# Five small moves of work in a hybrid decoder block: row factors, y operands, MLP operands, a refill

## The chip, the core and the metric

The kernel runs on one core of a Trainium2 chip. The metric is the device time of one execution in microseconds (us). A core has TensorE (PE in the profile, with its weight loads as PEld), VectorE (DVE), ScalarE (ACT), GpSimd (POOL) and SyncE (SP), which work side by side and wait for each other by semaphores, and 16 DMA engines. Matrix products land in PSUM. Each engine runs its own instructions in their order, so an instruction that waits holds up all that stand behind it on that engine.

## The reference

One decoder layer on x of 1 x 2048 x 1024 in float32; W_in has 3584 columns, the MLP 4096 hidden columns.

```python
h = rmsnorm(x, norm_mix_g)
u = h @ w_in                                  # split into gate_b, gate_c, v, x_r, g
y_conv = gate_b * causal_dwconv(gate_c * v, conv_w)
xr = causal_dwconv(x_r, rnn_conv_w) + rnn_conv_b
r = sigmoid(block_diag(xr, w_a) + b_a);  i = sigmoid(block_diag(xr, w_x) + b_x)
log_a = -8 * r * softplus(-lambda);  a = exp(log_a)
s_t = a_t * s_(t-1) + sqrt(1 - a_t^2) * i * xr          # the RG-LRU, a scan over time
y_rnn = s * gelu(g)
x = x + concat[rmsnorm(y_conv, g_norm_conv), rmsnorm(y_rnn, g_norm_rnn)] @ w_out
x = x + square(relu(rmsnorm(x, norm_mlp_g) @ w_mlp_in)) @ w_mlp_out
out = rmsnorm(x, final_norm_g)
```

## The kernel before

**Precision.** Every large product is made from three passes over operands split into a high and a low part: `round_off` makes the high part by a cast on ScalarE (L172) and the low part by a subtraction on VectorE (L173). So each weight tile and each activation tile costs one instruction on each of the two engines before TensorE can use it. Names end in `_hi` and `_lo`; an operand of the MLP is called `H`.

**Halves and stages.** The 2048 rows are worked in two halves of two blocks of 512 rows (`b = 0` and `b = 2` in the loop of `block_kernel`). Each half has the same stages:

1. The input projection and the two mixers. For b = 0 this is `mixers_plain`, product by product; for b = 2 `mixers_blocks`, where seven block products stand for eight (Strassen's way; the products are called 1, 2, 6, 5, 7, 3, 4 in the order in which they are run). The RG-LRU comes in units of 128 columns (`Lru`: `conv`, `gate`, `scan`, `out`). `Late` holds the last unit of a pair, whose gate and scan are put off into the next product; `between` runs these steps for the last pair of all, inside the next stage.
2. The output projection: `w_out_conv` for the rows' convolution part (twice, for the two row blocks), then `OutRows` for the recurrent part. Products go into PSUM tiles `po`; VectorE adds them to x (`add_rows`, tile x from po, L1231).
3. The MLP's first product: `Up`, 56 block products counted by `n`, with the seven operands H of 1, 2, 6, 5, 7, 3, 4. Results leave PSUM into `snap` tiles by ScalarE copies or VectorE adds (L1069, L1078).
4. The MLP's second product: `Down` (tile dn), and the last norm.

**The start.** The rows' norm factors are known only after squares of x have been summed. They are turned into a row of factors (`firsts[k].factors()`), spread over 128 partitions by a matmul of a diagonal with ones (`diag`, `bc`, L370), and copied into `R` by ScalarE (L405). `drain_x` (L720) and `drain_g` (L723) multiply product results by R on VectorE and so free their PSUM tiles: start_x and ps_x for x, ps_g for g. `col_products` makes the 48 matmuls of one column block against one block of rows and takes a function `halfway`, which it calls between them; the second spread already goes that way. The stores of kept weights (`d_ws`, on POOL's queue) are released by R (`issue_after(seen)`).

**The y operands.** y of the convolution part is stored in `d_yA`, fetched by `fetch_y` (tile y, two row blocks apart) and split by `conv_operands` into y_hi (ScalarE, L652) and y_lo (VectorE, L653).

**What sets the order.** On TensorE the order is the program's own from the first w_out on (`manual_schedule`) and in `mixers_blocks`; in `mixers_plain`, and on all other engines throughout, a scheduler orders instructions, with the code's order as its base. The PSUM pool has four tiles of 128 x 2 x 512. SP's queue carries most loads and some stores, POOL's queue the stores `d_ws`, `d_wk`, `d_u`, ACT's queue the stores `d_y`.

Of the kernel before, what the change touches and what calls it, by code (L numbers as in the profile page):

```python
# [61 lines left out]
def block_kernel(  # L62
# [618 lines left out]
    def mixers_plain(h):  # L681
        mix = Mix()
        late = None
        nxt = [Rows(2 + k, rs_next[:, k, :]) for k in range(2)]
        us = {}
        R = temp("R")
        R2 = None

        def over(t, blk):
            return t[:, blk : blk + 1, :].broadcast_to([P, 2, TB])  # L690

        def both(nm, drain, blks=range(2), w=None):
            w = w or take(nm)
            for blk in blks:
                drain(blk, col_products(nm, w, h[blk]))
            return w

        def around(nm, drain, steps):
            w = both(nm, drain, (0,))
            if steps:  # L700
                if nm == "c0":
                    late.u0.gate(late.gw)
                    late.u0.scan()
                else:
                    late.gate()
            both(nm, drain, (1,), w)
            if nm == "c0":
                late.gate()
            if steps:
                late.scan()  # L710

        for n in SEQUENCE:
            if n < 4:
                pr = n
                u0, u1 = Lru(2 * pr), Lru(2 * pr + 1)
                xin = new_xin(pr)
                g = wide("g")

                def drain_x(blk, ps):
                    V.tensor_mul(block(xin, blk, 3), ps, over(R, blk))  # L720

                def drain_g(blk, ps):
                    V.tensor_mul(block(g, blk), ps, over(R, blk))  # L723
                    nc.scalar.activation(block(g, blk), block(g, blk), AF.Gelu_apprx_tanh)

                if pr == 0:
                    pss = []
                    wg = both("g0", lambda blk, ps: pss.append(ps), (0,))
                    with tc.issue_after(prepare_second()):
                        for k in range(4):  # L730
                            firsts[0].part(k)
                    firsts[0].factors()
                    both("x0", lambda blk, ps: pss.append(ps), (1,), w_first)
                    psR = psum("bc")
                    firsts[0].spread(R[:, 0, :], psR[:, 0, :])
                    seen = nc.gpsimd.tensor_copy(warm, R[:, 0, 0:1]).ins
                    with tc.issue_after(seen):
                        for m, i, pair in held:
                            kept[m, i] = [spill_r("ws", t, nc.gpsimd) for t in pair]
                    split_kept = spilled[0]  # L740
                    drain_x(0, start_x)
                    for k in range(4):
                        firsts[1].part(k)
                    firsts[1].factors()
                    pss.append(
                        col_products(
                            "g0", wg, h[1], lambda: firsts[1].spread(R[:, 1, :], psR[:, 1, :])
                        )
                    )
                    drain_x(1, pss[1])  # L750
                    drain_g(0, pss[0])
                else:
                    around("x%d" % pr, drain_x, late)
                    wg = None
                gw = load_gate(pr)
                keep_halo(pr, xin)
                u0.conv(xin)
                if late:
                    late.out()
                if pr == 3:  # L760
                    fetched = [fetch_y(mix.ys["A"], q, 0) for q in range(2)]
                if pr:
                    wg = both("g%d" % pr, drain_g, (0,), take("g%d" % pr, 1 + pr // 3))
                u1.conv(xin)
                last = latest[0]
                if pr == 3:
                    keep_sums(n)
                    rA = stats(mix.acc["A"], 512, "A")
                if pr:
                    both("g%d" % pr, drain_g, (1,), wg)  # L770
                else:
                    drain_g(1, pss[2])
                if pr == 3:
                    ysA = conv_operands(fetched)
                if pr:
                    u0.gate(gw)
                    u0.scan()
                late = Late(mix, u0, u1, g, gw)
                if pr < 3:
                    with tc.issue_after(last), tc.issue_after(split_kept):  # L780
                        keep_sums(n)
                continue
            if n < 6:
                pr = n - 4
                if R2 is None:
                    R2 = temp("R2")
                    nc.scalar.activation(R2, R, AF.Square)
                gc = wide("gc")
                around(
                    "c%d" % pr,  # L790
                    lambda blk, ps: V.tensor_mul(block(gc, blk), ps, over(R2, blk)),
                    late,
                )
                if late:
                    late.out()
                    late = None
                cv = new_cv(pr)
                both(
                    "v%d" % pr,
                    lambda blk, ps: V.tensor_mul(block(cv, blk, 2), ps, block(gc, blk)),  # L800
                )
                u = conv_short(pr, cv)
                for blk in range(2):
                    V.tensor_mul(block(u, blk), block(u, blk), over(R, blk))
                us[pr] = spill("u", u, nc.gpsimd)
                for k in range(4):
                    nxt[pr].part(k)
                nxt[pr].factors()
            else:
                for pr in range(2):  # L810
                    u = refill_u(us[pr])
                    around(
                        "b%d" % pr, lambda blk, ps: V.tensor_mul(block(u, blk), ps, block(u, blk)), late
                    )
                    if late:
                        late.out()
                        late = None
                    mix.conv(u)
            keep_sums(n)

        def between(t):
            if t == 0:
                late.gate()
                late.scan()
            if t == 1:
                late.out()

        return mix, rA, ysA, between
# [100 lines left out]
    class InGate(In):  # L929

        def drain(self, i):
            def gated(u, blk, a):
                V.tensor_mul(block(u, blk), a, block(u, blk))

            def snap(t, ps):
                nc.scalar.copy(t, ps)
                return t

            def plus(t, ps):
                V.tensor_add(t, ps, t)  # L940
                return t

            if i == 1:
                self.u0 = refill_u(self.us[0])
                self.t = wide("snap")
                snap(block(self.t, 0), self.x)
            elif i == 2:
                gated(self.u0, 0, plus(block(self.t, 0), self.y))
            elif i == 6:
                self.u1 = refill_u(self.us[1])  # L950
                snap(block(self.t, 1), self.x)
            elif i == 5:
                snap(block(self.t, 0), self.w)
            elif i == 7:
                gated(self.u1, 1, plus(block(self.t, 0), self.x))
            elif i == 3:
                gated(self.u0, 1, plus(block(self.t, 1), self.w))
            elif i == 4:
                gated(self.u1, 0, self.x)
# [377 lines left out]
    for b in range(0, NB, 2):  # L1337
# [8 lines left out]
        with tc.manual_schedule(engines={nc.tensor.engine}):  # L1346
# [1 line left out]
            ahead = 0 if b else 1  # L1348
            ws = [take("oA0", ahead), take("oA1", ahead)]

            nextA = []

            def during(t):
                if t == 0:
                    nextA.extend(fetch_y(mix.ys["A"], q, 1) for q in range(2))
                between(t)
                if t == 0:
                    ysA.extend(conv_operands(nextA))
                if t == 2:
                    load_unit(cursor[0])  # L1360
# [75 lines left out]
        with tc.manual_schedule(engines={nc.tensor.engine}):  # L1436
# [6 lines left out]
            for n in range(-LEAD1, len(seq)):  # L1443
# [26 lines left out]
                    rest(2, xs[0])  # L1470
                if n == 1:
                    rest(3, xs[1])
                if n == 2:
                    for q in range(2):
                        V.tensor_tensor(raw1[q], raw1[2 + q], raw1[q], SUB)
                    ops.put(ops.begin(7), raw1[:2])
                if n == 3:
                    ops.put(ops.begin(3), raw1[2:])
                if n == 4:
                    ops.put(ops.begin(4), raw0[2:])  # L1480
                if s == NS - 1 and i in (5, 7, 3, 4):
                    m = (5, 7, 3, 4).index(i)
# [128 lines left out]
```

## Time and profile before

| | |
|---|---|
| Time, median of 3 runs | 2160.62 us (2160.02 to 2161.12) |
| The profiled execution | 2160.86 us, span 2159.1 us |
| Busy: PE | 2125.7 us, 9488 matmuls |
| Busy: DVE, ACT, POOL | 1481.7, 966.7, 184.8 us |
| DMA | 472.51 MB, mean 219 GB/s |

The span is the time from the first to the last record of the profiled execution, and all times of the timeline count from its start. A row of the timeline has the start in us, the busy us, the engine, the line of the code, the operation with the tiles out<-in, the shape and the number of instructions in the row; in brackets stands the idle time of the engine ahead of it, with the instruction that ended it. A row of the waits has total us, times and the longest. A row of the windows has the stretch, its length, the busy us of PE, PEld, DVE, ACT and POOL, the granted clock of PE (1.00 is full), the share of the DMA engines and GB/s. A matmul of 128 x 512 is shown as 0.39 us long, but the next starts before it ends.

### The profile page before, as it was taken

The page shows a single profiled execution, that of the slowest core. Times are in us where ns is not written, and L with a number is a line of the kernel's source. Part 1 is how long each engine was busy: PE and PEld are TensorE (multiplying, and loading weights), DVE is VectorE, ACT ScalarE, POOL GpSimd, SP SyncE. Part 2 cuts the span into 40 slices and gives each one's busy share as a digit, 9 for nine tenths or more (in the row PEclk, how much of TensorE's full clock was granted, in tenths as well). Part 3 has the DMA queues.
Part 4 walks back from the last instruction along what each step waited for, and adds up shares of the span by engine and source line. Part 5 has one row for each costly group of instructions (what it writes and reads, how often), then busy time and mean ns, then how long its engine had stood idle before and what let it go on. Part 6 is the DMA issues. An engine that isn't in the chain of part 4 may idle for free. (4 is left out here: it accounts for less than half of the span.)

```text
span 2159.1 us, 25110 instructions
## 1 busy us (share of the span) xinstructions
PE 2125.7 (98%) x9488; PEld 1745.3 (81%) x9488; DVE 1481.7 (69%) x1726; ACT 966.7 (45%) x1218; POOL 184.8 (9%) x335
## 2 busy tenths in 40 slices
PE   9999999999999999999999999999999999999998
PEld 7888887887888878888887887778888888888886
DVE  5887877569787876577746567595886665644456
ACT  6745537354333234453536447474533233433333
POOL 1121210000111100000121121000000000000000
PEclk9999999999999999999999999999999999999999
DMA  8755755342887789699573574654144444876431
GB/s 294 292 201 211 279 188 176 128 156 95 298 307 257 285 335 409 260 401 336 191 256 107 189 265 159 241 185 166 49 161 161 156 156 176 338 290 228 157 137 78
DMA packets 180904, 472.51 MB, mean 219 GB/s; under 512 B 15664, under 2 KB 62768, under 8 KB 179760
## 3 DMA queue, kind: packets, MB, share of 16 engines
q1 hardware_dynamic: 141104, 328.30, 42.0%
q0 software_dynamic: 36800, 133.19, 16.5%
q10 hardware_dynamic: 2880, 9.44, 1.2%
q8 instruction: 74, 1.21, 0.2%
q14 instruction: 46, 0.38, 0.0%
HBM read 308.33 MB, written 162.53 MB: 218 GB/s over the span
## 5 line engine op out<-in xcount | busy, mean ns | idle before, releaser
L870 PE MATMUL up<-H,w_hi 128*128 128x512 f32 x1792 | 552.5, 390 | 4.2 <-DVE snap L1078 3.4
L173 DVE TENSOR_TENSOR w_lo<-w,w_hi 128x1024 fp32r<-128x1024 f32 x208 | 253.2, 1222 | 273.8 <-issue 170.9
L870 PEld LDWEIGHTS up<-H,w_hi 128*128 128x128 f32 x1792 | 335.6, 188 | 74.8 <-ACT H L172 4.2
L1172 PE MATMUL dn<-w_lo,z_hi 128*128 128x512 f32 x896 | 348.8, 389 | 2.0 <-DVE w_lo L173 2.0
L1172 PE MATMUL dn<-w_hi,z_hi 128*128 128x512 f32 x896 | 349.2, 390 | 1.6 <-DVE x L1549 1.6
L870 PE MATMUL up<-H,w_lo 128*128 128x512 f32 x896 | 348.6, 389 | 0.0
L1172 PE MATMUL dn<-w_hi,z_lo 128*128 128x512 f32 x896 | 348.6, 389 | 0.0
L172 ACT CAST z_hi<-z 128x1024 fp32r<-128x1024 f32 x112 | 117.9, 1053 | 260.9 <-PE dn L1172 244.7
L172 ACT CAST w_hi<-w 128x1024 fp32r<-128x1024 f32 x208 | 216.0, 1049 | 30.2 <-DVE w L1051 14.6
L870 PE MATMUL in<-H,wr 128*128 128x512 f32 x888 | 203.2, 390 | 0.4 <-ACT g L892 0.4
L1172 PEld LDWEIGHTS dn<-w_lo,z_hi 128*128 128x128 f32 x896 | 168.2, 188 | 38.0 <-DVE w_lo L173 2.8
L1172 PEld LDWEIGHTS dn<-w_hi,z_hi 128*128 128x128 f32 x896 | 168.2, 188 | 37.8 <-DVE x L1549 2.4
L870 PEld LDWEIGHTS up<-H,w_lo 128*128 128x128 f32 x896 | 168.2, 188 | 35.2
L1172 PEld LDWEIGHTS dn<-w_hi,z_lo 128*128 128x128 f32 x896 | 168.2, 188 | 34.6
L870 PEld LDWEIGHTS in<-H,wr 128*128 128x128 f32 x888 | 166.4, 188 | 36.0 <-ACT g L892 0.8
L173 DVE TENSOR_TENSOR z_lo<-z,z_hi 128x1024 fp32r<-128x1024 f32 x112 | 136.6, 1219 | 19.9 <-ACT z_hi L172 18.6
L1065 ACT COPY snap<-up 128x1024 f32<-128x1024 f32 x48 | 48.8, 1016 | 184.6 <-PE up L870 184.6
L258 PE MATMUL po<-w_hi,y_hi 128*128 128x512 f32 x384 | 122.1, 400 | 4.0 <-ACT w_hi L172 3.0
L258 PE MATMUL po<-w_hi,y_lo 128*128 128x512 f32 x384 | 120.0, 394 | 3.3 <-DVE y_lo L653 3.3
L258 PE MATMUL po<-w_lo,y_hi 128*128 128x512 f32 x384 | 119.9, 394 | 0.2 <-DVE w_lo L173 0.2
L173 DVE TENSOR_TENSOR w_lo<-raw,w_hi 128x1024 fp32r<-128x1024 f32 (+1 forms) x62 | 73.1, 1186 | 47.9 <-issue 25.3
L172 ACT CAST w_hi<-raw 128x1024 fp32r<-128x1024 f32 (+1 forms) x62 | 62.7, 1019 | 88.4 <-PE ps_x L235 23.8
(265 smaller groups left out, 3088.7 us busy)
## 6 DMA issues: line engine op xcount, KB each, us to landing
z<-d_z SPq DMA_DIRECT2D x112, 512.0 KB, 7.4
w<-in_w_mlp_out_dram SPq DMA_DIRECT2D x80, 512.0 KB, 6.1
wr<-d_ws POOLq DMA_DIRECT2D x74, 512.0 KB, 6.4
w<-in_w_mlp_in_dram SPq DMA_DIRECT2D x64, 512.0 KB, 4.9
d_z<-snap SPq DMA_DIRECT2D x64, 512.0 KB, 3.0
w<-d_w SPq DMA_DIRECT2D x64, 512.0 KB, 4.7
d_z<-z SPq DMA_DIRECT2D x48, 512.0 KB, 2.9
d_ws<-w_hi POOLq DMA_DIRECT2D x37, 512.0 KB, 6.8
```

The source lines that it names most:

```text
L172: nc.scalar.copy(hi, src)
L173: latest[0] = V.tensor_tensor(lo, src, hi.bitcast(F32), SUB).ins
L258: nc.tensor.matmul(ps[:, half, :], ys[:, j, t * P : (t + 1) * P], ws[j][:, 0, half * 512 : (half + 1) * 512], start=first and i == 0, stop ...
L870: nc.tensor.matmul(ps[:, j, :], ws[:, k, j * P : (j + 1) * P], hs(k), start=i in (1, 2, 5) and k == 0 and n == 0, stop=k == 3 and n == len ...
L1065: nc.scalar.copy(t, ps)
L1172: nc.tensor.matmul(ps[t // 2][:, t % 2, :], zs[:, p, t * P : (t + 1) * P], ws[:, p, :], start=i in (1, 2, 5) and a == 0 and p == 0 and n == 0,
```

## The change

Of the five pieces that it is named for, four stand in the diff. The first spread of the row factors moves into the second row block's x product. In the first half's first w_out, the next y are split ahead of `between`. In the MLP, the operands of products 7, 3 and 4 are made behind block products 3, 5 and 6 and not 2, 3 and 4. In the gate's drain, the refill of the second u moves from product 6 to product 5, which is run right behind it. For the last LRU units' buffers, both files have the same line.

```diff
@@ mixers_plain, the first pair
                     firsts[0].factors()
-                    both("x0", lambda blk, ps: pss.append(ps), (1,), w_first)
                     psR = psum("bc")
-                    firsts[0].spread(R[:, 0, :], psR[:, 0, :])
+                    pss.append(
+                        col_products(
+                            "x0",
+                            w_first,
+                            h[1],
+                            lambda: firsts[0].spread(R[:, 0, :], psR[:, 0, :]),
+                        )
+                    )
                     seen = nc.gpsimd.tensor_copy(warm, R[:, 0, 0:1]).ins
@@ the gate's drain
             elif i == 6:
-                self.u1 = refill_u(self.us[1])
                 snap(block(self.t, 1), self.x)
             elif i == 5:
+                self.u1 = refill_u(self.us[1])
                 snap(block(self.t, 0), self.w)
@@ block_kernel, the first w_out_conv
-            nextA = []
 
             def during(t):
                 if t == 0:
-                    nextA.extend(fetch_y(mix.ys["A"], q, 1) for q in range(2))
+                    nextA = [fetch_y(mix.ys["A"], q, 1) for q in range(2)]
+                    if not b:
+                        ysA.extend(conv_operands(nextA))
                 between(t)
-                if t == 0:
+                if t == 0 and b:
                     ysA.extend(conv_operands(nextA))
@@ block_kernel, Up
-                if n == 2:
+                if n == 3:
                     for q in range(2):
                         V.tensor_tensor(raw1[q], raw1[2 + q], raw1[q], SUB)
                     ops.put(ops.begin(7), raw1[:2])
-                if n == 3:
+                if n == 5:
                     ops.put(ops.begin(3), raw1[2:])
-                if n == 4:
+                if n == 6:
                     ops.put(ops.begin(4), raw0[2:])
```

What the change does to the engines' orders is shown at three places. In the changed file lines move down by 6 behind the first edit and by 7 behind the MLP's.

At the start, TensorE, where ps_x is followed by ps_g (h_379 to h_386 are the second row block's parts). Before:

```order
L235 MATMUL ps_x<-h_385,w_hi 128x512
L235 MATMUL ps_x<-h_386,w_hi 128x512
L235 MATMUL ps_x<-h_385,w_lo 128x512
L370 MATMUL bc<-diag,ones 128x512
L235 MATMUL ps_g<-h_367,w_hi 128x512
L235 MATMUL ps_g<-h_368,w_hi 128x512
```

Now:

```order
L235 MATMUL ps_x<-h_379,w_lo 128x512
L370 MATMUL bc<-diag,ones 128x512
L235 MATMUL ps_x<-h_379,w_hi 128x512
L235 MATMUL ps_x<-h_380,w_hi 128x512
L235 MATMUL ps_x<-h_379,w_lo 128x512
L235 MATMUL ps_x<-h_385,w_hi 128x512
L235 MATMUL ps_x<-h_386,w_hi 128x512
L235 MATMUL ps_x<-h_385,w_lo 128x512
L235 MATMUL ps_x<-h_385,w_hi 128x512
L235 MATMUL ps_x<-h_386,w_hi 128x512
L235 MATMUL ps_x<-h_385,w_lo 128x512
L235 MATMUL ps_g<-h_367,w_hi 128x512
```

The matmuls of the first spread (bc) moved ahead of the last nine of ps_x. The second bc moved too, from behind 24 matmuls of the ps_g that follows to behind 41.

At the same place, ScalarE (xq are squares, rs_s the root for the second row block's factors). Before:

```order
L397 ACTIVATE xq,s_1_115<-xq 128x512 x2
L325 ACTIVATE rs_s<-rs_a 128x4
L405 COPY R<-bc 128x512
L172 CAST gate<-gate_raw 128x256
L724 ACT_TABLE_LOAD
L724 ACTIVATE g<-g 128x2x512
L172 CAST w_hi<-raw 128x1024 x2
L405 COPY R<-bc 128x512
```

Now:

```order
L405 COPY R<-bc 128x512
L397 ACTIVATE xq,s_1_115<-xq 128x512 x2
L724 ACT_TABLE_LOAD
L724 ACTIVATE g<-g 128x2x512
L325 ACT_TABLE_LOAD
L325 ACTIVATE rs_s<-rs_a 128x4
L172 CAST w_hi<-raw 128x1024
L172 CAST gate<-gate_raw 128x256
L172 CAST w_hi<-raw 128x1024
L405 COPY R<-bc 128x512
L172 CAST w_hi<-raw 128x1024
L724 ACT_TABLE_LOAD
```

The root for the second factors moved behind the first gelu (L724), and there are two more table loads.

In the first w_out of the first half, VectorE (x<-po are the drains, gi, xr and r the last unit's gate). Before:

```order
L535 TENSOR_SCALAR r<-xr 128x1024
L1231 SCALAR_TENSOR_TENSOR x<-po,yr_A,x 128x512
L536 SCALAR_TENSOR_TENSOR xr<-xr 128x1024
L530 TENSOR_TENSOR gi<-gi,xr 128x1024
L1231 SCALAR_TENSOR_TENSOR x<-po,yr_A,x 128x512 x2
L538 TENSOR_TENSOR gi<-gi,xr 128x1024
L539 SCALAR_TENSOR_TENSOR xr<-r,state,gi 128x1024
L544 TENSOR_TENSOR gi<-xr,g 128x1024
L653 SCALAR_TENSOR_TENSOR y_lo<-y,prm,y_hi 128x512
```

Now:

```order
L535 TENSOR_SCALAR r<-xr 128x1024
L653 SCALAR_TENSOR_TENSOR y_lo<-y,prm,y_hi 128x512
L536 SCALAR_TENSOR_TENSOR xr<-xr 128x1024
L653 SCALAR_TENSOR_TENSOR y_lo<-y,prm,y_hi 128x512 x3
L1237 SCALAR_TENSOR_TENSOR x<-po,yr_A,x 128x512
L538 TENSOR_TENSOR gi<-gi,xr 128x1024
L1237 SCALAR_TENSOR_TENSOR x<-po,yr_A,x 128x512
L539 SCALAR_TENSOR_TENSOR xr<-r,state,gi 128x1024
L1237 SCALAR_TENSOR_TENSOR x<-po,yr_A,x 128x512
L544 TENSOR_TENSOR gi<-xr,g 128x1024
L530 TENSOR_TENSOR gi<-gi,xr 128x1024
```

The four y_lo moved ahead of a drain of po, and the second unit's gi (L530) behind the first unit's scan (L539). On ScalarE the four y_hi stand ahead of the second unit's gate in the same way.

In the MLP's start of each half, VectorE (raw_3506 and raw_3507 make the operand H of product 7; numbers are of the first half). Before:

```order
L1048 TENSOR_TENSOR s_3897<-w_3502,w_3524 128x1024
L1475 TENSOR_TENSOR raw_3506<-raw_3508,raw_3506 128x1024
L1049 TENSOR_TENSOR w_3524<-w_3524 128x1024
L1475 TENSOR_TENSOR raw_3507<-raw_3509,raw_3507 128x1024
L1051 TENSOR_TENSOR w_3502<-w_3524,w_3502 128x1024
L173 TENSOR_TENSOR H_3932<-raw_3506,H_3930 128x1024
L173 TENSOR_TENSOR H_3933<-raw_3507,H_3931 128x1024
L173 TENSOR_TENSOR w_lo<-w_3521,w_hi 128x1024
L1078 TENSOR_TENSOR snap<-up,snap 128x1024
```

Now:

```order
L1054 TENSOR_TENSOR s_3897<-w_3502,w_3524 128x1024
L1482 TENSOR_TENSOR raw_3506<-raw_3508,raw_3506 128x1024
L1055 TENSOR_TENSOR w_3524<-w_3524 128x1024
L173 TENSOR_TENSOR w_lo<-w_3521,w_hi 128x1024
L1057 TENSOR_TENSOR w_3502<-w_3524,w_3502 128x1024
L1084 TENSOR_TENSOR snap<-up,snap 128x1024
L1482 TENSOR_TENSOR raw_3507<-raw_3509,raw_3507 128x1024
L1075 SCALAR_TENSOR_TENSOR snap<-snap 128x1024
L173 TENSOR_TENSOR H_3965<-raw_3506,H_3963 128x1024
L173 TENSOR_TENSOR H_3966<-raw_3507,H_3964 128x1024
```

The snap (L1078, now L1084) moved ahead of one raw and of both H. Where the refill of u stands (SP's rows of u from d_u), no engine's order has changed.

## The prediction, made before the changed kernel had run

> **What bounds the kernel now.** I read the busy table of the page first, then the waits of TensorE (PE), then the granted clock, then the timeline around each wait that the change touches.
>
> ```profile
> span 2159.1 us, 25110 instructions
> PE 2125.7 (98%) x9488; PEld 1745.3 (81%) x9488; DVE 1481.7 (69%) x1726; ACT 966.7 (45%) x1218; POOL 184.8 (9%) x335
> ```
>
> PE is busy for 98% of the span and the change leaves its 9488 matmuls as they are, so only PE's idle time, and time at a lower clock, can be won or lost. The idle time has names:
>
> ```profile
> PE up L870 <- DVE snap L1078: 3.4, 2, 1.7
> PE po L258 <- DVE y_lo L653: 3.3, 3, 1.9
> PE po L258 <- ACT w_hi L172: 3.0, 1, 3.0
> PE dn L1172 <- DVE w_lo L173: 2.0, 1, 2.0
> PE ps_g L235 <- DVE xr_in L720: 2.0, 1, 2.0
> ```
>
> Columns: total us, times, longest. Edit 3 touches the first row, edit 2 the second, edit 1 the fifth: 8.7 us together. The windows view gives the granted clock (PEclk) in the stretch after that fifth wait, and in two others:
>
> ```profile
> 44.00:49.00 5.00, 4.97 (x15) 3.99 (x16) 2.29 (x7) 2.72 (x4) 2.51 (x5) 0.66 1.00 392
> ...
> 392.00:398.00 6.00, 5.49 (x23) 4.56 (x24) 1.91 (x15) 1.46 (x3) 0.00 (x0) 0.72 0.41 121
> 1386.00:1394.00 8.00, 6.79 (x16) 4.96 (x17) 5.77 (x5) 5.05 (x5) 0.00 (x0) 0.57 0.26 84
> ```
>
> At 0.66 for 5 us, (1 − 0.66) × 5 = 1.7 us are lost beside the 2.0 idle.
>
> **Edit 1, the first spread.** R, the row factors' copy, is made from a bc matmul. R feeds xr_in on VectorE (DVE), which frees the PSUM buffer that ps_g wants. The timeline of PE, then of ACT, then of DVE around it:
>
> ```profile
> 37.84 0.39 PE L235 MATMUL ps_x<-h,w_hi 128*128 128x512 f32 x1
> ...
> 40.78 0.40 PE L235 MATMUL ps_x<-h,w_lo 128*128 128x512 f32 x1
> 41.02 1.02 PE L370 MATMUL bc<-diag,ones 128*128 128x512 f32 x2
> 44.03 0.72 PE L235 MATMUL ps_g<-h,w_hi 128*128 128x512 f32 x2 [1.99 <-DVE xr_in L720]
> ...
> 51.21 1.02 PE L370 MATMUL bc<-diag,ones 128*128 128x512 f32 x2
> ...
> 57.54 0.39 PE L235 MATMUL ps_c<-h_hi,w_hi 128*128 128x512 f32 x1
> 42.13 0.59 ACT L405 COPY R<-bc 128x512 f32<-128x512 f32 x1 [6.42 <-PE bc L370]
> ...
> 34.37 0.62 ACT L397 ACTIVATE xq<-xq 128x512 f32<-128x512 f32 x1
> 45.21 1.06 ACT L724 ACTIVATE g<-g 128x1024 f32<-128x1024 f32 x1 [0.89 <-DVE g L723]
> 42.75 1.22 DVE L720 TENSOR_TENSOR xr_in<-start_x,R 128x1024 f32<-128x1024 f32 x1 [6.23 <-ACT R L405]
> ...
> 45.10 0.86 DVE L362 TENSOR_SCALAR diag<-ident,rs_x 128x128 f32<-128x128 f32 x4
> ...
> 51.23 2.36 DVE L173 TENSOR_TENSOR w_lo<-raw,w_hi 128x1024 fp32r<-128x1024 f32 x2 [4.94 <-issue]
> ```
>
> Thirteen matmuls lie between 37.84 and 40.78: 0.226 us each at full clock. The order of the changed kernel has 9 ps_x matmuls behind bc, so bc starts 9 × 0.226 = 2.0 us earlier, at 39.0. The same chain (copy 1.1 after bc starts, xr_in 0.6 later, 1.22 long) then ends at 41.9, and PE has finished ps_x and bc at 42.0 (44.03 − 1.99): the idle goes. I take the 1.7 of low clock as going with it, since it stands right behind it. Together 3.7; PE drains a little at the changeover, 0.2. Gain 3.5, ps_c at 54.0. If the low clock stays, the gain is 1.8.
>
> The cover is thinner behind it: bc's second matmul group moves from behind 24 ps_g matmuls to behind 41, so to 42.0 + 41 × 0.226 = 51.3. Its diag must be there. ScalarE (ACT) now runs the R copy to 40.7, two squares (34.37: 0.62 each) to 42.0, the gelu table, g (1.06), the sqrt table back, and the root that the factors need: 42.0 + 1.28 + 1.06 + 1.28 = 45.6 (a table load is 1.28 in the next fence). These are two table loads more than before. VectorE's small steps take about 1 us, then diag pieces alternate with two w_lo (1.2 each), which want ps_g's 24th matmul (47.5) done: diag complete at about 50.5, 0.8 us ahead of PE. If that cover is gone, PE waits by the excess. The Trainium skill, "ScalarE: Activation LUTs", What ACT_TABLE_LOAD costs, says that every switch costs about 1.28 us for the load and 1.38 us for a drain, 2.66 in all; two switches would bring the diag to about 53.3, a wait of 2.0 on PE, and edit 1 would be worth 1.5 by it, an estimate. The trace agrees on the load and shows less of a drain: the activation stands 0.01 us behind the load in the next fence (343.29 + 1.28, then 344.58).
>
> The kept weights' stores are released by R as well, so they leave 2 us earlier with it. No wait of PE stands in the waits view that they would end.
>
> **Edit 2, y operands in the first w_out.** In the first half (b = 0) the four next y are split ahead of the last unit's gate instead of between its steps. The DMA view of the fetch (KB each, us to landing), then the timeline of ACT, PE and SP's queue:
>
> ```profile
> y<-d_yA SPq DMA_DIRECT2D x4, 256.0 KB, 7.7
> 343.29 1.28 ACT L533 ACT_TABLE_LOAD   x1
> 344.58 1.15 ACT L533 ACTIVATE r<-r,sp 128x1024 f32<-128x1024 f32 x1
> ...
> 350.43 1.11 ACT L523 ACTIVATE gi<-psri,prm 64x1024 f32<-64x1024 f32 x1
> ...
> 356.29 0.71 ACT L652 ACTIVATE y_hi<-y,prm 128x512 fp32r<-128x512 f32 x1
> 359.62 0.73 PE L258 MATMUL po<-w_hi,y_lo 128*128 128x512 f32 x2 [1.23 <-DVE y_lo L653]
> ...
> 363.15 0.73 PE L258 MATMUL po<-w_hi,y_lo 128*128 128x512 f32 x2 [1.88 <-DVE y_lo L653]
> ...
> 351.88 0.62 PE L258 MATMUL po<-w_hi,y_hi 128*128 128x512 f32 x2
> 337.80 2.30 SPq L127 DMA_DIRECT2D y<-d_yA  x4
> ```
>
> The four loads go out between 337.8 and 340.1; with 7.7 us each they land between 345.5 and 348. Now y_hi follows the r of 344.58: four of 0.7, 345.75 to 348.7. VectorE's y_lo follow each, done by 352. PE wants the first at 358.4 (359.62 − 1.23), so all three waits go: 3.3 idle, and about 0.15 more for each restart (below), 3.7. What is late next: the gate (table, r, gi, r, gi) runs after y_hi and a root, to 356.9 instead of 351.5, and PSUM comes free later. PE wants the next buffer at the 351.88 row; VectorE, which does three y_lo ahead of that drain, gives it at about 352.6: a new wait of 0.7. Gain 3.0. If that buffer is the gate's instead, PE waits for the second gi, at about 354.7, 2.8 us, and the gain is 0.9.
>
> **Edit 3, MLP operands 7, 3, 4, in both halves.** VectorE makes the H of block product 7 right ahead of the snap that frees PSUM. The timeline of DVE, then of PE, and a later row of DVE:
>
> ```profile
> 501.40 1.22 DVE L1475 TENSOR_TENSOR raw<-raw,raw 128x1024 f32<-128x1024 f32 x1
> ...
> 505.94 2.35 DVE L173 TENSOR_TENSOR H<-raw,H 128x1024 fp32r<-128x1024 f32 x2
> 508.21 1.22 DVE L173 TENSOR_TENSOR w_lo<-w,w_hi 128x1024 fp32r<-128x1024 f32 x1
> 509.35 1.22 DVE L1078 TENSOR_TENSOR snap<-up,snap 128x1024 f32<-128x1024 f32 x1
> 508.62 0.39 PE L870 MATMUL up<-H,w_lo 128*128 128x512 f32 x1
> 510.71 0.70 PE L870 MATMUL up<-H,w_hi 128*128 128x512 f32 x2 [1.70 <-DVE snap L1078]
> 528.87 1.23 DVE L1048 TENSOR_TENSOR s<-w,w 128x1024 f32<-128x1024 f32 x1 [3.74 <-DMA w<-in_w_mlp_in_dram]
> ```
>
> The start-to-start loss is 510.71 − 508.62 − 0.23 = 1.86, 0.16 over the idle shown. In the new order one raw and the two H stand behind the snap. The two H hold VectorE from 505.94 to 508.21, 2.27, and a raw half of that: the snap starts 3.4 earlier, at 505.9, ends at 507.1, and PE wants the buffer at 508.85. The wait goes with 1.7 to spare, and its twin in the second half too (the waits row has two, 3.4 together): 2 × 1.85 = 3.7. The H pieces come later. H of 7 should be ready by about 512, of 3 by 520, of 4 by 524; at 11 us a block product, PE uses 7 first at about 525 and 4 at 536. So these cost nothing, short of the cover of over 10 us going. The next w_lo may come up to 0.3 late at about 560, in each half; I count 0, and 0.6 as the other end.
>
> **Edit 4 and the fifth piece.** Moving the refill of u in the loop leaves every engine's and queue's order and waits in that region as they were: 0. The fifth, the last units' buffers, has no line in the diff: 0.
>
> **The sum.** 3.5 + 3.0 + 3.7 = 10.2. The profiled execution took 2160.86 us, 1.8 around its span and 0.24 over the median of 2160.62. Against the first it gives 2150.7, against the median 2150.4. I say 2150.5.
>
> **The rivals.** *New waits take most of it.* The diag is 2 us late and brings back the low clock (edit 1 worth −0.2), and PSUM waits for the gate (edit 2 worth 0.9); with the 0.6 at edit 3 the sum is −0.2 + 0.9 + 3.1 = 3.8: 2156.8. One of the two alone leaves 6.5 to 8: 2152.5 to 2154. For it: 0.8 us of cover. Against: every term behind that 0.8 is a measured row.
>
> *The gain is absorbed.* If the two waits on w_lo and w_hi in the second fence end at a fixed time because loads arrive then, everything earlier is lost there; only the second half of edit 3 is behind both: 1.9, 2158.7. For it: VectorE waits for loads of weights in the MLP (528.87). Against: these loads are issued as buffers come free, which PE paces, so they move too.
>
> *The clock goes another way.* Two other low-clock stretches cost 1.7 and 3.4 us by the windows above, (1 − 0.72) × 6 and (1 − 0.57) × 8, the latter in part its idle. If the shift in time takes PE past them, 3 to 5 more are won: about 2146.5. Against: the idle stays. Other waits of 1.7 to 1.9 us (363.15, 510.71) have no low clock behind them, so it is partly a matter of when. The Trainium skill, "TensorE: Matmul & The Clock Gate", Part 1: The HAM clock gate, has the clock halve after an idle window of about 3.4 us that runs freely; by it no wait here is long enough, and edit 1 would have no low clock to win. The trace, 0.66 behind 1.99 idle, does not bear that out.
>
> *Slower.* The last unit's y is stored and fetched again late, since its gate runs later:
>
> ```profile
> 372.82 0.33 ACTq L131 DMA_DIRECT2D d_y<-gi  x1
> ...
> 387.89 1.38 ACT L652 ACTIVATE y_hi<-y,prm 128x512 fp32r<-128x512 f32 x2 [2.92 <-DMA y<-d_y]
> ```
>
> I put the store about 5.7 later, at 378.5; with 2.6 for its landing and 2.6 for the fetch (my estimate, from DMA times at this place in the trace) the last y is there at about 384, against PE's need 3 us earlier than now, at about 388: it holds with about 1 us left after the splits. Each us beyond costs PE one. Slower by 0.2% needs 10.2 + 4.3 lost there, so a store 15 us later still: if the scan chain were held behind the whole column block. Then about 2166.
>
> **How the numbers follow.** 0.2%, 4.3 us, is about what a measurement of this kernel tells from no change. The forecast 0.68; one new wait 0.10; two 0.05; absorbed 0.07; the clock's luck 0.06; slower 0.04. The forecast's own terms have ends of 1.8 to 3.5, 0.9 to 3.7 and 3.1 to 3.7, so 2149.7 to 2154.8; I reach below to the clock's luck, 2145.5, and above to the bound of faster, 2156.3, which leaves out the double wait, the absorbed and the slower case, 0.16. Faster: 0.68 + 0.10 + 0.06 = 0.84; same: 0.05 + 0.07 = 0.12; slower 0.04.
>
> **What would show it.** Right: ps_g starts by 42.2 with no idle and PEclk at 1.0 behind it; ps_c at about 54; no wait on y_lo around 356 and one under 1 us on a drain of po about 7 us earlier; no wait on snap L1078 (L1084 in the new numbering) at about 505 and 1555; PE's total idle down by some 8. Wrong: a wait of PE on diag near 51, on gi near 351, or on a late y near 385; waits on w_lo or w_hi at the starts of Down and of the second w_out that have grown.

## The result, and the profile after

| | median us | runs | against before |
|---|---|---|---|
| before | 2160.87 | 4 | |
| after | 2149.51 | 4 (2147.82 to 2153.81) | 0.9947 (0.9931 to 0.9963) |
| before, beside e5 | 2159.89 | 23 | |
| after, once more (e5) | 2149.07 | 6 | 0.9945 (0.9932 to 0.9958) |

The change makes the kernel about 11 us faster; 10.2 were forecast. The profiled execution of after took 2147.82 us, 13.0 less than the profiled one of before, so the two traces show about 2 us more than the medians do. The ratios leave out three disturbed executions: 7641.73 us in e1, 2366.12 in e5 and 10180.74 in e8. The page of after:

```profile
span 2146.0 us, 25111 instructions
PE 2123.7 (99%) x9488; PEld 1746.1 (81%) x9488; DVE 1480.2 (69%) x1726; ACT 969.0 (45%) x1220; POOL 184.7 (9%) x335
```

The waits of TensorE in after, with the same columns as before:

```profile
PE po L258 <- ACT w_hi L172: 3.0, 1, 3.0
PE psri L509 <- DVE xr_lo L173: 1.8, 2, 1.0
PE dn L1178 <- DVE x L1556: 1.6, 2, 0.8
...
PE po L258 <- DVE x L1237: 0.7, 1, 0.7
```

The rows on snap L1078, on y_lo and on xr_in are gone, and one of 0.7 on a drain of po is new. Two more rows of before are gone, whose going the prediction did not forecast: the 2.0 on w_lo at the start of Down, and this one, on the snap L1086 near 707:

```profile
PE up L870 <- DVE snap L1086: 0.7, 1, 0.7
```

All rows of PE's waits together come to 24.4 us in before and 13.4 in after.

Laying each matmul of after beside the same one of before gives where the 13.0 us lie: +1.2 at the start (from 3 to 8 us 28 matmuls fall where before has 41; this differs from run to run), −3.6 by ps_c, −2.9 over the first w_out, −2.0 at each of the two snap waits, −3.4 in the first half's MLP from about 565 to 797, and −0.4 at a wait of statistics near 1449.

At the start, the timeline of PE in after:

```profile
40.18 1.02 PE L370 MATMUL bc<-diag,ones 128*128 128x512 f32 x2
...
42.89 0.39 PE L235 MATMUL ps_x<-h,w_lo 128*128 128x512 f32 x1
43.19 0.74 PE L235 MATMUL ps_g<-h,w_hi 128*128 128x512 f32 x2
...
52.67 1.02 PE L370 MATMUL bc<-diag,ones 128*128 128x512 f32 x2
...
55.15 0.39 PE L235 MATMUL ps_c<-h_hi,w_hi 128*128 128x512 f32 x1
```

and the timeline of ACT there:

```profile
43.13 1.28 ACT L724 ACT_TABLE_LOAD   x1
44.43 1.06 ACT L724 ACTIVATE g<-g 128x1024 f32<-128x1024 f32 x1
45.51 1.28 ACT L325 ACT_TABLE_LOAD   x1
46.80 0.21 ACT L325 ACTIVATE rs_s<-rs_a 128x4 f32<-128x4 f32 x1
```

ps_g starts 0.30 us behind the last ps_x, 0.07 more than the 0.226 of one matmul to the next. Each table load is followed by its activation 0.01 to 0.02 us after its end. The windows of after, at the start and at the two later stretches of low clock:

```profile
44.00:49.00 5.00, 5.00 (x23) 4.13 (x22) 1.80 (x10) 4.96 (x7) 1.76 (x4) 1.00 1.00 389
...
385.00:395.00 10.00, 9.49 (x43) 7.86 (x42) 5.65 (x19) 3.87 (x6) 0.00 (x0) 0.83 0.67 229
1376.00:1386.00 10.00, 9.53 (x30) 6.92 (x32) 5.63 (x6) 4.31 (x5) 0.00 (x0) 0.66 0.44 138
```

The low clock behind the first wait has gone; the two others stand. In the first w_out and at the MLP's start, DVE in after:

```profile
347.55 2.07 DVE L653 SCALAR_TENSOR_TENSOR y_lo<-y,prm,y_hi 128x512 fp32r<-128x512 f32 x3
349.54 0.74 DVE L1237 SCALAR_TENSOR_TENSOR x<-po,yr_A,x 128x512 f32<-128x512 f32 x1
...
500.59 1.22 DVE L1084 TENSOR_TENSOR snap<-up,snap 128x1024 f32<-128x1024 f32 x1
```

and PE:

```profile
350.33 0.73 PE L258 MATMUL po<-w_hi,y_hi 128*128 128x512 f32 x2 [0.71 <-DVE x L1237]
...
503.51 0.61 PE L876 MATMUL up<-H,w_hi 128*128 128x512 f32 x2
```

The three y_lo hold up one drain, and PE waits 0.71 for it. The snap that frees the MLP's buffer now ends at 501.81, 1.7 before PE comes to it at 503.51.

### The profile page after: what moved, and what is told of

Its sections match the earlier page's. It is cut to its first block, busy times and chain, and to the rows that moved or that the text cites. A ratio compares the mean times of both kernels' runs of the same rounds, so it can differ in the third digit from the quotient of the medians.

```text
span 2146.0 us, 25111 instructions
## 1 busy us (share of the span) xinstructions
PE 2123.7 (99%) x9488; PEld 1746.1 (81%) x9488; DVE 1480.2 (69%) x1726; ACT 969.0 (45%) x1220; POOL 184.7 (9%) x335
## 3 DMA queue, kind: packets, MB, share of 16 engines
q8 instruction: 74, 1.21, 0.2%
```

## The experiments

Two theories. The first: each edit is worth its own waits, and these add up to the result. The second: there is more in the result than the waits named, since the loads and sums of the second MLP weights (`w2_sums`) changed as well, and the gains of different places depend on each other. The runs of the kernel before beside each set have medians of 2160.05 (33 runs), 2159.89 (23) and 2160.10 (27). The standard deviation of one run is 2 us (the 83 runs lie between 2155.3 and 2165.8), so ratios carry about 0.1%, 2 us. The brackets are 95% intervals.

**e1, edit 1 alone.** The change's first hunk (a hunk is one block of the diff), nothing else.

> Only the first spread is moved into the x product (edit 1); all else as before. Theory: the 1.99 us wait on xr_in and the low clock behind it go, -3.6 us, so about 2157.2; the waits of the MLP's first half (snap L1078 1.70 near 510, snap L1086 0.70 near 707, w_lo 2.03 near 797) stand as before. Rival: those later waits shrink because TensorE comes earlier, up to 2 us more, about 2155.

Measured: 2159.54 us, ratio 1.000 (0.9989 to 1.0011): no gain that can be seen, and 3.6 lies outside the interval. In its trace the local gain is there: counted from the first matmuls, ps_c comes 3.6 us earlier. Later it is given back. Windows of e1:

```profile
44.00:49.00 5.00, 5.00 (x23) 4.12 (x22) 1.80 (x10) 4.00 (x6) 1.54 (x3) 1.00 1.00 387
361.00:366.00 5.00, 5.00 (x16) 3.59 (x15) 4.57 (x7) 1.06 (x1) 0.00 (x0) 0.66 0.55 189
1450.00:1455.00 5.00, 5.00 (x16) 3.91 (x16) 4.56 (x15) 3.22 (x5) 0.00 (x0) 0.66 0.71 247
```

and the waits of its MLP:

```profile
PE dn L1178 <- DVE w_lo L173: 3.2, 1, 3.2
```

Two other stretches run at low clock, 1.7 us lost in each, at places where the profile of before has full clock:

```profile
363.00:368.00 5.00, 4.69 (x19) 3.60 (x20) 5.00 (x8) 1.06 (x1) 0.00 (x0) 1.00 0.83 297
1450.00:1455.00 5.00, 5.00 (x22) 4.15 (x23) 5.00 (x15) 3.80 (x7) 0.00 (x0) 1.00 0.64 217
```

And the wait on w_lo is 1.2 longer. The later waits did not shrink, so the rival fails as well.

**e2, edit 2 alone.** The change's hunk in the first w_out.

> Only the y operands of the first half's first w_out are split early (edit 2). Theory: the three waits on y_lo (3.3 us idle, 3.9 by start times) go, one wait of about 0.7 on a drain of po comes, -2.8 us, about 2158.0; the waits near 510, 707 and 797 stand. Rival: they shrink, to about 2156.

Measured: 2160.07 us, ratio 1.0001 (0.9992 to 1.0011). The trace has the three waits gone and the new one of 0.7. The expected 2.8 lies outside this interval too. The theory's figure fails here as at e1.

**e3, edit 3 alone.** The three conditions on n.

> Only the MLP operands 7, 3 and 4 are made later (edit 3). Theory: the two waits on snap L1078 go (-3.7), and the waits near 565, 707 and 797 go with them (-3.5), because the loads of the second MLP weights stand earlier in SP's queue and the chain of their sums on VectorE starts earlier: -7.2 us, about 2153.6. Rival: the later waits went because the whole stage came earlier by edits 1 and 2; then they stand here, -3.7 us, about 2157.1.

Measured: 2154.99 us, ratio 0.9977 (0.9968 to 0.9986), −3.0 to −6.9 us. Both snap waits are gone. The waits on snap L1086 and on w_lo are still in its trace:

```profile
PE dn L1172 <- DVE w_lo L173: 1.5, 1, 1.5
PE up L870 <- DVE snap L1086: 0.7, 1, 0.7
```

So they do not go with edit 3; the theory's −7.2 is outside the interval, the rival's −3.7 inside.

**e4, edit 4 alone.**

> Only the refill of u is moved to product 5 (edit 4). The orders of all engines and queues are those of before, so both theories expect no difference: 2160.8 us, within 1 us. What it differs by shows what run to run noise does to a median.

Measured: 2159.29 us, ratio 1.0001 (0.9992 to 1.001). No effect. Its use is as a second look at the kernel before. The wait at the start is there, in PE's timeline:

```profile
44.80 0.73 PE L235 MATMUL ps_g<-h,w_hi 128*128 128x512 f32 x2 [1.99 <-DVE xr_in L720]
```

but the window behind it is at full clock, where before had 0.66:

```profile
45.00:50.00 5.00, 5.00 (x23) 4.13 (x23) 2.07 (x6) 2.78 (x4) 2.38 (x5) 1.00 1.00 392
```

The wait on w_lo at Down's start is 0.8 here, against 2.0. The engines' orders are the same in both traces, and yet they differ by 1.7 of low clock and 1.2 of wait, 2.9 us in things that nothing has changed.

**e5, all edits once more.**

> The changed kernel once more, with more runs and another profile. If the waits near 565, 707 and 797 (2.9 us before, none in the first profile after) went because of the change, they are absent here too and the median is some 11 us under before. Rival: they vary from run to run with the loads of the second MLP weights (2.7 us together in the profile before, 3.7, 2.3, 2.2 and 1.6 in the four single edits); then they are back here, up to 2 to 3 us, and the median is 8 to 9 under before.

Measured: 2149.07 us, ratio 0.9945 (0.9932 to 0.9958). A wait on w_lo is back in the MLP:

```profile
PE dn L1178 <- DVE w_lo L173: 1.6, 1, 1.6
```

The median is the one expected if the change had removed these waits (−11), the trace is the rival's: their absence in the first profile was in part chance.

**e6, edits 1, 2 and 4.** The change without the conditions on n.

> Edits 1, 2 and 4, without the MLP operands of edit 3. If gains add by TensorE's idle time: -2.0 -2.6 idle and nothing from the clock, -4.6 us. If the two single results (0.0 each) are all there is: 0 to -1 us. If the low clock at the start counts too: -6.4 us. The wait on snap near 505 stands, 1.7.

Measured: 2155.38 us, ratio 0.9976 (0.9967 to 0.9986), −3.1 to −7.1 us. Its trace is no better than e1's or e2's in the MLP:

```profile
PE up L876 <- DVE snap L1092: 2.7, 2, 2.4
PE dn L1178 <- DVE w_lo L173: 2.1, 1, 2.1
```

Together the two edits gain the 4.6 of their idle, apart they gained nothing that shows. With e3, −5.2 and −5.0 make −10.2, against −11 for all: these two parts add up.

**e7 and e8, the sums moved.** Each job of `w2_sums` one block product earlier, or later, on top of the change:

```diff
-                if more and n > 7 and n % 3 == 2:
-                    w2_sums(n // 3 - 2)
+                if more and 6 < n < 55 and n % 3 == 1:      # e7
+                    w2_sums(n // 3 - 2)
+                if more and n > 8 and n % 3 == 0:           # e8
+                    w2_sums(n // 3 - 3)
```

> The changed kernel with each job of the second MLP weights' sums (w2_sums) issued one block product earlier. If the last job's load, which VectorE waits for ahead of the first w_lo of Down, is what makes the wait near 797, that wait is gone in every run: 1 to 2 us less than the changed kernel. Rival: that wait comes from the first casts on ScalarE; then nothing changes.

> The changed kernel with each job of w2_sums issued one block product later. By the theory the last job's load lands up to 5.5 us later and TensorE waits on w_lo at Down's start for 3 to 6 us: slower than the changed kernel by that. Rival: no change.

Measured: e7 2152.26 us, ratio to before 0.9964 (0.9952 to 0.9976), about 3 us slower than the change alone; e8 2157.69 us, 0.999 (0.9981 to 1.0), some 8.5 slower. e8 agrees with the theory that a late last job makes TensorE wait, but loses more than the 3 to 6 expected. Its waits in the MLP's first half:

```profile
PE dn L1178 <- DVE w_lo L173: 3.0, 2, 2.4
PE up L876 <- DVE w_lo L173: 2.6, 1, 2.6
PE up L876 <- DVE snap L1092: 1.0, 1, 1.0
```

e7 does not agree, since 1 to 2 less than the change was expected: a wait of 1.6 on w_lo remains, and new ones of 0.9 stand in the middle of the stage. The jobs' place is not the whole cause.

**e9 and e10, edit 3 in one half.** The three conditions as `n == (3 if more else 2)` and so on (e9, first half alone), and the other way round (e10).

> Before, with the operands 7, 3 and 4 made later in the first half (b = 0) alone. There the loads of the second MLP weights also take other places in SP's queue. By the snap wait alone: -1.85 us. If the first half's chain of sums gains too (edit 3 alone gave some 5, of which the two snap waits explain 3.7): -3 to -3.5.

> Before, with the operands made later in the second half (b = 2) alone; SP's order is that of before and there are no sums of second weights in that half. Both theories: -1.85 us, the wait on snap near 1565 gone and nothing else.

Measured: e9 2157.91 us, 0.9984 (0.9975 to 0.9993); e10 2157.77 us, 0.9989 (0.998 to 0.9998). The intervals are −1.5 to −5.4 and −0.4 to −4.3: 1.85 fits both, and a larger gain in the first half is neither shown nor ruled out.

**e11, the sums' tiles from another pool.**

```diff
-        ts = [wtile("w2", (P, D)) for _ in range(2)]
+        ts = [temp("w2", (P, D)) for _ in range(2)]
```

> The changed kernel with the tiles of w2_sums taken from the pool of 23 buffers and not from that of 15. If the loads of these weights go out late because they wait for a buffer that VectorE's w_lo frees (SP waits 12.6 us on it between 730 and 790), they go out earlier, VectorE no longer waits for them, and the waits near 565, 707 and 797 are gone in the profile: 1 to 2 us less than the changed kernel. Rival: the loads are late for the DMA engines' sake or the scheduler's order; then no gain, or a loss of up to 3 us.

Measured: 2162.61 us, ratio 1.0014 (1.0005 to 1.0023): slower than before, and some 13 us slower than the change. In its trace the MLP's first half waits more:

```profile
PE up L876 <- DVE snap L1092: 7.1, 4, 3.0
PE dn L1178 <- DVE w_lo L173: 1.6, 2, 0.9
PE dn L1178 <- ACT w_hi L172: 1.3, 1, 1.3
```

The expected gain did not come, and the loss is larger than the rival's 3. The order on VectorE and on SP's queue changed with the pool, so the buffer was not tested by itself: whether these loads wait for want of one stays open.

**e12, the second y one step later.**

```diff
-                        ysA.extend(conv_operands(nextA))
+                        ysA.extend(conv_operands(nextA[:1]))
+                        later.extend(nextA[1:])
+                if t == 1 and later:
+                    ysA.append(split_y(later[0], "g_norm_conv", 2))
                 between(t)
```

> The changed kernel with the second y split one step later (behind the last unit's gate and ahead of its out), to take away the wait of 0.7 us on a drain of po that edit 2 brought. Expected: that wait is gone, -0.9 us. Rival: the second y's y_lo come late again behind the scan and a wait on y_lo of 1 to 2 us returns; two more table loads on ScalarE speak for it: +0 to +1.

Measured: 2149.19 us, ratio 0.9951 (0.9939 to 0.9964), the same as the change. Its waits:

```profile
PE dn L1178 <- DVE w_lo L173: 2.6, 1, 2.6
...
PE up L876 <- DVE snap L1092: 1.4, 1, 1.4
...
PE po L258 <- DVE y_lo L653: 0.7, 1, 0.7
```

The wait on the drain is gone and one as long on y_lo has come: the rival held, with 0.7 in place of its 1 to 2. In the MLP's first half all engines have the orders of the change, and here it waits 4.0 us, against 0 and 1.6 in the two profiles of the change. That settles that its sum varies from execution to execution. By profile, snap L1086 (L1092) and w_lo together: 2.7, 3.7, 2.3, 1.6, 4.8 and 2.2 without edit 3 in the first half (before, e1, e2, e4, e6, e10), mean 2.9; 2.2, 0, 0, 1.6 and 4.0 with it (e3, e9, after, e5, e12), mean 1.6. With so few profiles and such a spread that is a hint that edit 3 helps there, no more.

## Why the prediction was right, and where its steps were not

**Edit 1, the chain.** Right in place and size: no idle at ps_g, clock at 1.00 behind it, ps_c 3.6 earlier (counted from the matmuls behind the start, 1.2 late here) where 3.5 was said. The diag was complete at 51.8, 0.9 ahead of its bc at 52.67; 0.8 was said. The 0.2 that PE was to drain at the changeover shows in no run; ps_g came 0.07 late. The two added table loads took 1.28 each and no more; the drain of 1.38 that the Trainium skill ("ScalarE: Activation LUTs", What ACT_TABLE_LOAD costs) adds to a switch does not show here.

**Edit 1, the low clock.** This term, 1.7, was booked as won in full, and the step that failed is "I take the 1.7 of low clock as going with it". In the first pair of profiles it is there: ahead of the last matmul the trace of before has four stretches of 3.41 us at half clock (one of 6.83 counted as two), 1.7 us lost in each, and that of after three. On average it is not there:

- The wait was followed by low clock in four of the six profiles of kernels that have it (last section). So its going is worth 1.1 and not 1.7.
- Such stretches come elsewhere instead. The six profiles have 22 of them, 3.7 each, and the eight with edit 1 have 31, 3.9 each.
- The mean granted clock of a run says the same. Over 83 runs of the kernel before it is 0.9964, a loss of (1 − 0.9964) × 2158 = 7.8 us. (Some 2 us of it lie behind the last matmul: in the profile of before the clock is low from 2154.8 to the end, and the last matmul ends at 2150.3.) In nine runs of the change it is 0.996, 8.6 us, to about 1 us, since it is given to three places. In ten of e1 it is 0.9955, 9.7 us: 1.9 more than before, with a standard error of 0.9.

In the run as a whole edit 1 has thus not won its 1.7.

**Edit 2.** Right: the three waits went, and the one foreseen of 0.7 came, by the drain that was named, at the place that was named. −2.9 in the trace against −3.0. The last unit's gate ended at 354.5, which with the 2.4 us already won is the 356.9 of the prediction.

**Edit 3.** Right: both waits went, with 1.7 to spare as said, and no wait came near 560. Edit 3 alone gave −3.0 to −6.9, which holds the 3.7. The later H cost nothing: that of product 7 was complete at 506.4 and first used at 519.8. One figure of the prediction is wrong, without effect: a block product has 24 matmuls and takes 5.4 us, not 11.

**Edit 4 and the fifth piece.** Right: e4 measured nothing, and there was nothing of the fifth to measure.

**The sum.** 10.2 were forecast and 11 measured. PE's waits fell by 11.0 in the first pair of profiles and by 8.9 in e5, where some 8 was said. But the sum did not come by its terms alone: the clock's 1.7 shows in no mean, and waits in the first half's MLP that were counted as standing (2.7 us in the profile before) were 0 and 1.6 in the two profiles of the change. The two roughly cancel, so the forecast's size owes something to luck. The rival "the gain is absorbed" named the wait on w_lo at Down's start, and in e1 that wait was 1.2 longer, which is no more than it varies by itself (2.0 in before, 0.8 in e4); with all edits it did not grow. "Slower" had no part: no wait on a late y shows.

**Open.** Why edits 1 and 2 show nothing apart and about 5 us together is not settled. The clock can be part of it: by the runs' mean granted clock 1.9 us more than before are lost in e1, 1.0 in e2 and 0.9 in e6, each to some 0.8 (standard error). And the intervals of e1 and e2 reach to −2.4 and −1.7, together −4.1, which lies within e6's −3.1 to −7.1. How the 5 us are shared between the two edits was thus not measured. What paces the chain of the sums was not settled either: e7, e8 and e11 all made it worse. No version beat the change; e12 equals it.

## What to carry to other kernels

Where one engine is busy for 98% of the time, its waits, named and priced from one trace, forecast this change well; but count only idle time, and price a stretch at low clock by how often it follows the wait over several profiles. Lay the profile of an unchanged program beside a second one of itself before an effect of 1 to 3 us is read out of two traces. When work is moved ahead of a drain, price the one drain that it holds up: here that was the cost seen, and moving the work again only changed its name.

## What the runs showed of the hardware that was not expected

The same wait of 1.99 us at the start was followed by low clock (0.66 over 44 to 49) in four profiles, before, e2, e3 and e9, where it ended at 44.0 to 44.3, and by full clock in two, e4 and e10, where it ended at 44.8 and 45.0. The wait of 2.99 us on w_hi in the second half was followed by low clock in all 14 profiles. So a wait of 2 us can be enough, and whether it is hangs on when it falls. The clock's own records in the 14 traces show the pattern: between the first change of the clock and the last, every stretch at full or at half clock is a whole multiple of 3.41 us long, on a grid that starts at another moment in each execution. In the four profiles with low clock the whole wait of 1.99 lies inside one step of this grid, and the clock is halved for the next step (in before, the step from 41.93 to 45.34, then low to 48.76). In e4 and e10 the wait is split over two steps, 1.21 and 0.78, and 1.35 and 0.64, and the clock stays full. The Trainium skill, "TensorE: Matmul & The Clock Gate", Part 1: The HAM clock gate, has a free-running window of about 3.4 us and the clock halved after one idle window; the dependence on when and the step of 3.41 agree with a free-running window, while the length does not: 1.99 us were enough four times in six.
